# Gate and up of a SwiGLU by Strassen's seven products, their product through DRAM, on one Trainium2 core

## The chip, the cores and the metric

The kernel runs on one core of one Trainium2 chip. The metric is the device time of one execution in microseconds (us); less is better. Before the change the median of three runs is 2609.01 us (2608.06 to 2616.32). The core's engines are named as the profile names them: PE is TensorE's matmul, PEld its weight load, DVE is VectorE, ACT ScalarE, POOL GpSimd, and SP (SyncE) issues all the DMAs here.

## The reference

One layer of a block that mixes a state-space branch and a long convolution, then a feed-forward part; 512 tokens, width 2048, feed-forward width 5632, all in float32. The change is in the feed-forward part:

```python
def swiglu(h, wg, wu, wd):
    return (jax.nn.silu(h @ wg) * (h @ wu)) @ wd

        x = x + g1 * rmsnorm(y, norm_mix_post[layer])
        h = modulate(x, norm_ffn_pre[layer], sh2, sc2)
        x = x + g2 * rmsnorm(swiglu(h, w_gate[layer], w_up[layer], w_down[layer]), norm_ffn_post[layer])
```

## The kernel before, in words

Everything is kept transposed: features on the 128 partitions, the 512 tokens along the free dimension. A matrix product runs in three matmuls of type float32r: each operand is split into a high part and the rest, and `mm3` (L185) adds high x high, high x low and low x high into one PSUM bank of 512 columns (`acc`, four banks).

**Weights.** `wload` (L159) loads 128 x 1024 numbers (eight stationary blocks of 128 x 128) by a DMA on SP into `raw` (L156, three buffers), ACT casts them to `whi` (L164) and DVE subtracts to get `wlo` (L79); three buffers each, of 4096 bytes a partition, in the pool wp. `push` (L193) loads the weights of one step at once and runs the matmuls of the step two pushes earlier, so two steps of weights are ahead of PE. `gemm` (L212) pushes two such halves for a tile of 128 outputs and 2048 inputs. Between groups of four stationary blocks it calls `pump` (L136), which runs `pace` steps of generators in `fillers`: small work of DVE, ACT and POOL that is laid between the matmuls.

**Moving operands.** The pool big has 32 tiles of 512 columns (2048 bytes a partition), h0 to h15 and l0 to l15, used in turn for the inputs of all projections (hh, hl; mh, mlo) and then for the feed-forward input fx (`fh`, `fl`). By these sizes a moving operand and its weights begin at the same place of a 128-byte grid. `wload_big` (L168) puts weights that are used twice into tiles of big.

**The stretch around the change.** The output projection of the mixer ends in `y_second` (L1212), first for tokens 0 to 255, then for 256 to 511. After each half a filler `junction` (L1190) norms and adds (yT is then the stream x after the mixer, kept to the end of the kernel), norms again, and writes that half of fx (`modulated`, L302). Then come gate and up. `gate_up(i, c0, c1)` (L1248) makes tile i of 44: 96 matmuls for gate, 96 for up, silu on ACT, product on DVE, split into `ah` and `al` (six tiles of each, NA = 6, in the pool fa). The first six tiles run in two halves of 256 tokens, since the second half of fx comes later. After that chunks of four tiles (NCHUNK = 11) alternate with `down` (L1281): for each of eight q, two output tiles of 512 columns take the chunk's four inputs, and DVE adds each result into `y2a` (ACT copies the first). `ada(1)` between tiles runs one step of a matrix-vector product on DVE whose weights are loaded through `raw` as well. The last chunk runs in two halves of 256 tokens, with most of its weights kept by `wload_big`; `finish` (L1306) norms, adds yT and stores.

**Order.** The kernel is written in the Tile framework, which puts in the waits and plans the order of each engine's instructions and of SP's DMAs; an engine then takes its own in that order, and an instruction that waits holds up those behind it on its engine.

Of the kernel before, what the change touches and what calls it, by code (L numbers as in the profile page):

```python
# [23 lines left out]
EPS = 1e-6  # L24
NA = 6
LEAD = 2
NSQ = 0
# [37 lines left out]
def block_kernel(ctx: ExitStack, tc: tile.TileContext, I: dict, out: bass.AP, dbg=None, stop=None):  # L65
# [32 lines left out]

    rsm.tile([128, 16], F32, name="pad1")
    uniq = [0]  # L100
# [24 lines left out]

    hh = [big.tile([128, 512], F32R, tag=f"h{k}", name=f"hh{k}") for k in range(KT)]
    hl = [big.tile([128, 512], F32R, tag=f"l{k}", name=f"hl{k}") for k in range(KT)]
    hx = [(hh[k], hl[k]) for k in range(KT)]
# [39 lines left out]
    def wload_big(ap, q):  # L168

        raw = wraw(ap)  # L170
        parts = []
        for i in range(2):
            o = i * 512
            hi = big.tile([128, 512], F32R, tag=f"h{q * 2 + i}", name=nm("bhi"))
            lo = big.tile([128, 512], F32R, tag=f"l{q * 2 + i}", name=nm("blo"))
# [882 lines left out]
    flush(I["w_out"][n, 0] for n in range(2))  # L1058
    mh = [big.tile([128, 512], F32R, tag=f"h{k}", name=f"mh{k}") for k in range(KT)]
    mlo = [big.tile([128, 512], F32R, tag=f"l{k}", name=f"ml{k}") for k in range(KT)]  # L1060
    for j in range(8):
# [108 lines left out]

    fa_cm = pool("fa")
    fa = fa_cm.__enter__()
    jn_cm = pool("jn", side="right")
    jn = jn_cm.__enter__()
    posc = fa.tile([128, 512], F32, tag="ah", bufs=NA, name="posc")
    pos = pos_load(jn, posc.rearrange("p (k c) -> p k c", k=8))
    xr = [jn.tile([128, 512], F32, name=f"xr{k}") for k in range(KT)]
# [12 lines left out]
    def junction(h, prs):  # L1190
# [3 lines left out]
        for k in range(KT):  # L1194
            stt(yT[k][:, sl], yT[k][:, sl], gp[:, k : k + 1], rx[:, sl], MUL, MUL)
            tt(nc.vector if k % 2 else nc.gpsimd, yT[k][:, sl], yT[k][:, sl], xr[k][:, sl], ADD)
            pr2.add(yT[k][:, sl])
            yield
        yield
        yield from rstd_steps(pr2, D, 2, rx[:, sl])  # L1200
        for k in range(KT):
            if h == 0:
                fx[k] = (big.tile([128, 512], F32R, tag=f"h{k}", name=f"fh{k}"),
                         big.tile([128, 512], F32R, tag=f"l{k}", name=f"fl{k}"))
            modulated(fx[k][0][:, sl], fx[k][1][:, sl], yT[k][:, sl], a2[:, k : k + 1], mod[:, 5, k : k + 1], rx[:, sl], 256)
            yield
# [38 lines left out]

    acts = {}

    def gate_up(i, c0, c1):  # L1248
# [3 lines left out]
        def up_done(pu):  # L1252
            if i not in acts:
                h = fa.tile([128, 512], F32R, tag="ah", bufs=NA, name=nm("ah"))
                l = fa.tile([128, 512], F32R, tag="al", bufs=NA, name=nm("al"))
                acts[i] = (h, l)
# [15 lines left out]
    jn_cm.__exit__(None, None, None)  # L1272
    ff_cm = pool("ff")
    ff = ff_cm.__enter__()
    y2a = ff.tile([128, 16, 512], F32, name="y2a")
    y2 = [y2a[:, n, :] for n in range(16)]
    pace[0] = 1
    for i in range(NA):
        gate_up(i, 256, 512)

    def down(c, q, c0, c1, done, w=None):  # L1281
        def run(wt):
            for s in range(2):
                n = q * 2 + s
                p = acc()[:, : c1 - c0]
                for k in range(4):
                    ah, al = acts[c * 4 + k]
                    mm3(p, *wt[s * 4 + k], ah[:, c0:c1], al[:, c0:c1], k == 0, k == 3)
                if c == 0:
                    nc.scalar.copy(out=y2[n][:, c0:c1], in_=p)  # L1290
                else:
                    tt(nc.vector, y2[n][:, c0:c1], y2[n][:, c0:c1], p, ADD)
                done(n)
# [3 lines left out]

    for c in range(NCHUNK):
        for i in range(max(c * 4 + NA - 4, NA), min(c * 4 + NA, 44)):
            gate_up(i, 0, 512)  # L1300
        for q in range(8 if c < NCHUNK - 1 else 0):
            down(c, q, 0, 512, lambda n: None)
    ada(1000)
    tt(nc.vector, gp, mod[:, 7, :], vec[:, V_FPOST : V_FPOST + 16], MUL)

    def finish(h, prs):  # L1306
        sl = slice(h * 256, h * 256 + 256)
        yield from rstd_steps(prs, D, 2, rx[:, sl])
        for n in range(0, 16, FG):
            y = y2a[:, n : n + FG, sl]  # L1310
            tt(nc.vector, y, y, rx[:, sl].unsqueeze(1).broadcast_to([128, FG, 256]), MUL)
            tt(nc.gpsimd if n // FG % FP in FQ else nc.vector, y, y, yTa[:, n : n + FG, sl], ADD)
            nc.sync.dma_start(out[n : n + FG, :, sl].rearrange("n p t -> p n t"), y)
# [22 lines left out]
    drain()  # L1336
    ff_cm.__exit__(None, None, None)
    fa_cm.__exit__(None, None, None)
    yt_cm.__exit__(None, None, None)

# [116 lines left out]
```

## Time and profile before

| what | value |
|---|---|
| median of three runs | 2609.01 us |
| profiled execution, its own time | 2608.6 us |
| its span, first to last instruction | 2606.8 us |
| mean granted clock of PE | 0.981 |
| PE busy | 2512.0 us (96%) |
| PEld busy | 2054.6 us (79%) |
| DVE busy | 1471.9 us (56%) |
| ACT busy | 759.4 us (29%) |
| POOL busy | 456.2 us (18%) |
| DMA | 388.52 MB, mean 149 GB/s |

Busy time is how long an engine had an instruction in it; matmuls overlap, so a row's mean of one matmul is longer than the distance between two starts. The chain of waits goes back from the last instruction to what released each step. [...]

### The profile page before, as it was taken

The numbers are of one execution on the slowest core, as the hardware profiler recorded it, in microseconds if no ns is written. First come the engines' busy times: TensorE is split into PE (matmuls) and PEld (weight loads), VectorE is DVE, ScalarE is ACT, GpSimd is POOL, SyncE is SP. The second block draws the span as 40 slices with busy tenths as digits, with TensorE's granted clock in tenths as the row PEclk, the third lists the DMA queues.
The fourth block names the chain that finished last, engine by engine and source line by source line (L and its number), as shares of the span: only waits on it lengthen the run. The fifth ranks groups of instructions, "written<-read, shape, count | busy, mean of one in ns | idle before, by whom it ended". The sixth has DMA issues, their size and how long they took to land.

```text
span 2606.8 us, 30938 instructions
## 1 busy us (share of the span) xinstructions
PE 2512.0 (96%) x12196; PEld 2054.6 (79%) x12196; DVE 1471.9 (56%) x1889; ACT 759.4 (29%) x1062; POOL 456.2 (18%) x421
## 2 busy tenths in 40 slices
PE   8999989899999999999999999999999999999997
PEld 3467779577767789999988888888888888888886
DVE  7986746888878767696334343434343333333335
ACT  3143325222123323455322222222222222222224
POOL 1130010665523245740000000000000000000005
PEclk9999999899999999999999999999999999999998
DMA  8867744444356666345433333333333333333332
GB/s 290 315 225 236 235 156 161 143 149 162 113 197 215 249 222 220 105 146 184 148 113 112 108 113 113 113 113 113 113 113 105 97 97 98 97 97 97 97 106 73
DMA packets 129354, 388.52 MB, mean 149 GB/s; under 512 B 13775, under 2 KB 34703, under 8 KB 127672
## 3 DMA queue, kind: packets, MB, share of 16 engines
q1 hardware_dynamic: 129208, 386.54, 45.3%
q8 instruction: 96, 1.57, 0.3%
q14 instruction: 50, 0.41, 0.0%
HBM read 367.09 MB, written 19.40 MB: 148 GB/s over the span
## 4 chain that ended last, share of the span: by engine, by line
PE 55%; DVE 2%; POOL 0%; issue 0%; ACT 0%; POOLq 0%; ACTq 0%; DVEq 0%
PE acc L82 55%; DVE y2a L79 1%; DVE yTa L76 0%; POOL gs L79 0%; PE aux L236 0%; PE aux L82 0%; DVE wlo L79 0%; DVE yTa L79 0%; ACT sq L73 0%; ACT whi L164 0%; POOLq L1452 0%; POOL r L79 0%; ACT dg L73 0%; POOL yTa L79 0%; ACT rx L279 0%
## 5 line engine op out<-in xcount | busy, mean ns | idle before, releaser
L164 ACT CAST whi<-raw 128x1024 fp32r<-128x1024 f32 (+1 forms) x436 | 453.2, 1040 | 1410.5 <-PE acc L82 1156.5
L79 DVE TENSOR_TENSOR wlo<-raw,whi 128x1024 fp32r<-128x1024 f32 x420 | 533.2, 1269 | 540.3 <-ACT whi L164 536.2
L82 PE MATMUL acc<-fh,wlo 128*128 128x512 f32 (+1 forms) x1600 | 583.2, 365 | 4.1 <-DVE wlo L79 4.1
L82 PE MATMUL acc<-fh,whi 128*128 128x512 f32 (+1 forms) x1600 | 583.6, 365 | 0.1
L82 PE MATMUL acc<-fl,whi 128*128 128x512 f32 (+1 forms) x1600 | 583.1, 365 | 0.0
L82 PEld LDWEIGHTS acc<-fh,wlo 128*128 128x128 f32 x1600 | 303.3, 190 | 51.9 <-DVE wlo L79 4.7
L82 PEld LDWEIGHTS acc<-fh,whi 128*128 128x128 f32 x1600 | 303.3, 190 | 47.9 <-ACT fh L73 0.3
L82 PEld LDWEIGHTS acc<-fl,whi 128*128 128x128 f32 x1600 | 303.3, 190 | 47.6 <-DVE fl L76 0.2
L79 POOL TENSOR_TENSOR gs<-gs,sq 128x256 f32<-128x256 f32 x91 | 86.7, 956 | 1432.1 <-ACT sq L73 1430.1
L82 PE MATMUL acc<-hh,whi 128*128 128x512 f32 x688 | 283.9, 415 | 4.3 <-ACT hh L73 4.1
L82 PE MATMUL acc<-hl,whi 128*128 128x512 f32 x688 | 276.9, 402 | 2.8 <-DVE hl L76 2.8
L82 PE MATMUL acc<-hh,wlo 128*128 128x512 f32 x688 | 274.9, 400 | 0.0
L76 DVE SCALAR_TENSOR_TENSOR ada<-raw,cc,ada 128x512 f32<-128x512 f32 x240 | 199.1, 830 | 114.4 <-DMA raw<-in_ada 111.1
L82 PE MATMUL acc<-ah,whi 128*128 128x512 f32 (+1 forms) x688 | 262.7, 382 | 0.0
L82 PE MATMUL acc<-ah,wlo 128*128 128x512 f32 (+1 forms) x688 | 262.5, 382 | 0.0
L82 PE MATMUL acc<-al,whi 128*128 128x512 f32 (+1 forms) x688 | 262.4, 382 | 0.0
L79 DVE TENSOR_TENSOR y2a<-y2a,acc 128x512 f32<-128x512 f32 (+1 forms) x176 | 112.1, 638 | 199.6 <-PE acc L82 199.4
L82 PEld LDWEIGHTS acc<-hh,whi 128*128 128x128 f32 x688 | 133.1, 194 | 40.1 <-ACT hh L73 6.0
L82 PEld LDWEIGHTS acc<-hh,wlo 128*128 128x128 f32 x688 | 133.0, 193 | 33.9 <-issue 4.5
L82 PEld LDWEIGHTS acc<-hl,whi 128*128 128x128 f32 x688 | 133.1, 193 | 33.8 <-DVE hl L76 3.8
L82 PEld LDWEIGHTS acc<-ah,whi 128*128 128x128 f32 x688 | 129.3, 188 | 25.2
L82 PEld LDWEIGHTS acc<-al,whi 128*128 128x128 f32 x688 | 129.3, 188 | 25.0
(297 smaller groups left out, 3084.1 us busy)
## 6 DMA issues: line engine op xcount, KB each, us to landing
raw<-in_ada SPq DMA_DIRECT2D x128, 512.0 KB, 3.8
raw<-in_w_gate SPq DMA_DIRECT2D x100, 512.0 KB, 3.5
raw<-in_w_up SPq DMA_DIRECT2D x100, 512.0 KB, 3.5
raw<-in_w_down SPq DMA_DIRECT2D x88, 512.0 KB, 3.5
ada<-in_ada SPq DMA_DIRECT2D x64, 512.0 KB, 5.0
raw<-in_w_hy SPq DMA_DIRECT2D x44, 512.0 KB, 3.8
raw<-in_w_out SPq DMA_DIRECT2D x41, 512.0 KB, 4.4
raw<-in_w_xbc SPq DMA_DIRECT2D x38, 512.0 KB, 3.3
```

The source lines that it names most:

```text
L76: nc.vector.scalar_tensor_tensor(out=o, in0=a, scalar=s, in1=b, op0=op0, op1=op1)
L79: e.tensor_tensor(out=o, in0=a, in1=b, op=op)
L82: nc.tensor.matmul(o, lhsT, rhs, start=start, stop=stop)
L164: nc.scalar.copy(out=hi[:, :n], in_=raw[:, :n])
```

## The change

**Gate and up by pairs of tiles.** The first six tiles stay as they are. The other 38 are taken in 19 pairs, gate and up each: a block of 256 outputs (two tiles) x 2048 inputs (two halves) times 2048 inputs x 512 tokens (two halves) is a 2 x 2 by 2 x 2 product of blocks. `quad` makes it in seven block products of 128 x 1024 by 1024 x 256, in the form with few additions, and not in eight. Four sums of the moving blocks are made once (`sums_of_x`, a filler beside the second halves of the first six tiles; split into th and tl), four sums of the weights for each block on DVE before the cast. The seven results lie in four PSUM banks; `early` and `end` combine them into R on DVE and ACT, then silu, then the product with gate.

**The product goes through DRAM.** It is stored to `hd` (also that of the first six tiles) and loaded again by `act_load` for down, two tiles a DMA, then split. yT is stored to `x1d` in the junction, its space is given to the sums and weights, and `finish` loads it again through three tiles.

**Down in three chunks.** Chunks 0 to 4 and 5 to 9 each are summed in PSUM over 20 inputs; chunk 10 runs as before. ada steps run in the first of these.

**Operands 64 bytes apart.** The tiles of big are 576 columns wide and used from column 16, fx from column 0; wp begins with a pad of 64 bytes; pads in rsm and fd follow. So fx, th and tl begin 64 bytes off their weights on the 128-byte grid, the other operands of big do not.

```diff
-    rsm.tile([128, 16], F32, name="pad1")
+    rsm.tile([128, 64], F32, name="pad1")
+    wp.tile([128, 16], F32, name="pad2")
...
+    def block(tag, name, o=16):
+        return big.tile([128, 576], F32R, tag=tag, name=name)[:, o : o + 512]
...
+            nc.sync.dma_start(x1d[k][:, sl], yT[k][:, sl])
             yield
...
-                fx[k] = (big.tile([128, 512], F32R, tag=f"h{k}", name=f"fh{k}"),
-                         big.tile([128, 512], F32R, tag=f"l{k}", name=f"fl{k}"))
+                fx[k] = (block(f"h{k}", f"fh{k}", 0), block(f"l{k}", f"fl{k}", 0))
...
-            split(acts[i][0][:, c0:c1], acts[i][1][:, c0:c1], sg[:, :n])
-            if n == 512:
-                ada(1)
+            nc.sync.dma_start(hd[i][:, c0:c1], sg[:, :n])
...
+    def sums_of_x():
+        for k in range(8):
+            xb = gu.tile([128, 4, 256], F32, tag="ra", bufs=4, name=nm("xb"))
+            tb = gu.tile([128, 4, 256], F32, tag="ra", bufs=4, name=nm("tb"))
+            for i, q in enumerate((k, k + 8)):
+                tt(nc.vector, xb[:, 2 * i : 2 * i + 2, :].rearrange("p a b -> p (a b)"),
+                   fx[q][0].bitcast(F32), fx[q][1].bitcast(F32), ADD)
+            yield
+            tt(nc.vector, tb[:, 0:4:2, :], xb[:, 1:4:2, :], xb[:, 0:2, :], SUB)
+            tt(nc.vector, tb[:, 1, :], xb[:, 3, :], tb[:, 0, :], SUB)
+            tt(nc.vector, tb[:, 3, :], tb[:, 1, :], xb[:, 2, :], SUB)
+            yield
+            th = gu.tile([128, 4, 256], F32R, tag=f"th{k}", name=f"th{k}")
+            tl = gu.tile([128, 4, 256], F32R, tag=f"tl{k}", name=f"tl{k}")
+            split(th, tl, tb)
+            tx.append((th, tl))
+            yield
...
+    def feed(raw, body):
+        hi = wp.tile([128, 1024], F32R, tag="whi", bufs=3, name=nm("whi"))
+        lo = wp.tile([128, 1024], F32R, tag="wlo", bufs=3, name=nm("wlo"))
+        nc.scalar.copy(out=hi, in_=raw)
+        if pend:
+            pend.pop()()
+        pend.append(lambda: tt(nc.vector, lo, raw, hi.bitcast(F32), SUB))
+        for op in late:
+            op()
+        late.clear()
+        ahead.append(([(hi[:, c : c + 128], lo[:, c : c + 128]) for c in range(0, 1024, 128)], body))
+        if len(ahead) > 2:
+            w, fn = ahead.pop(0)
+            fn(w)
...
+        def early():
+            p12, p75, p6 = ps[0], ps[2], ps[4]
+            nc.scalar.copy(out=R[:, 0, :], in_=p12[:, 0:256])
+            tt(nc.vector, R[:, 0, :], p6[:, 0:256], R[:, 0, :], SUB)
+            tt(nc.vector, R[:, 2, :], R[:, 0, :], p75[:, 0:256], SUB)
+            tt(nc.vector, R[:, 1:4:2, :], R[:, 0:4:2, :], p75[:, 256:512].unsqueeze(1).broadcast_to([128, 2, 256]), ADD)
+            nc.scalar.copy(out=R[:, 0, :], in_=p12[:, 0:256])
+            tt(nc.vector, R[:, 0, :], R[:, 0, :], p12[:, 256:512], ADD)
+
+        def end():
+            tt(nc.vector, R[:, 1:3, :], R[:, 1:3, :], ps[5].rearrange("p (a b) -> p a b", a=2), SUB)
...
+                tt(nc.vector, R[:, 0, :], R[:, 0, :], g[:, 0, :], MUL)
+                stt(R[:, 1, :], R[:, 1, :], -1.0, g[:, 1, :], MUL, MUL)
+                tt(nc.vector, R[:, 2:4, :], R[:, 2:4, :], g[:, 2:4, :], MUL)
+                nc.sync.dma_start(hd[m1 : m1 + 2].rearrange("m p t -> p m t"), R.rearrange("p (m a) b -> p m (a b)", m=2))
...
+        feed(r11, body(0))
+        feed(r12, body(1))
+        tt(nc.vector, r11, r11, r21, ADD)
+        feed(r11, body(2))
+        tt(nc.vector, r21, r21, r22, ADD)
+        feed(r21, body(3))
...
+        tt(nc.vector, r11, r11, r22, ADD)
+        feed(r11, body(4))
...
+        feed(r22, body(5))
+        tt(nc.vector, r11, r11, r12, ADD)
+        feed(r11, body(6))
...
+    def act_load(i):
+        raw = fd.tile([128, 2, 512], F32, tag="st", bufs=3, name=nm("st"))
+        nc.sync.dma_start(raw, hd[i : i + 2].rearrange("m p t -> p m t"))
+        for b in range(2):
...
+            split(h, l, raw[:, b, :])
+            acts[i + b] = (h, l)
...
+    for g, (ca, cb) in enumerate(((0, 5), (5, 10))):
...
+                if g == 0:
+                    ada(1)
+                down_piece(c, q, ps, c == ca, c == cb - 1, done)
...
+        x1 = [y2p.tile([128, FG, 256], F32, tag="x1", bufs=3, name=nm("x1"))]
+        nc.sync.dma_start(x1[0], x1d[0:FG, :, sl].rearrange("n p t -> p n t"))
```

`body(i)` runs the 24 matmuls of product i, each of 256 columns; each `feed` is one cast, one subtraction and the matmuls of the product two feeds earlier.

## Rows read from the trace of the kernel before

**Rows 1.** The page: busy time by engine, and the granted clock in 40 slices.
```profile
PE 2512.0 (96%) x12196; PEld 2054.6 (79%) x12196; DVE 1471.9 (56%) x1889; ACT 759.4 (29%) x1062; POOL 456.2 (18%) x421
...
PEclk9999999899999999999999999999999999999998
```

**Rows 2.** The chain that ended last: start us, us, what.
```profile
1168.70 298.10 PE acc L82 x1716
...
1467.58 261.29 PE acc L82 x1152
...
1991.73 567.37 PE acc L82 x2592
...
2591.54 9.92 DVE y2a L79 x11
```

**Rows 3.** Busy time of each engine by stretch, granted clock, DMA share, GB/s.
```profile
core 0: us, PE busy (x) PEld busy (x) DVE busy (x) ACT busy (x) POOL busy (x), PEclk, DMA share, GB/s
0.00:40.00 40.00, 33.58 (x64) 9.60 (x64) 25.76 (x44) 19.44 (x35) 4.74 (x9) 1.00 0.84 309
...
1151.00:1159.00 8.00, 4.44 (x32) 4.00 (x32) 8.00 (x10) 3.71 (x7) 7.20 (x8) 0.98 0.21 68
1159.00:1163.00 4.00, 4.00 (x24) 4.00 (x24) 3.62 (x6) 2.33 (x6) 1.42 (x2) 0.62 0.49 135
...
1190.00:1270.00 80.00, 80.00 (x669) 80.00 (x668) 42.15 (x50) 34.95 (x46) 0.00 (x0) 1.00 0.58 183
1270.00:2535.00 1265.00, 1265.00 (x5597) 1048.14 (x5597) 462.86 (x501) 292.31 (x326) 0.00 (x0) 1.00 0.34 106
```

**Rows 4.** Timeline of PE, matmuls of 256 columns: start us, us, what.
```profile
1119.62 0.28 PE L82 MATMUL acc<-fh,whi 128*128 128x256 f32 x1
...
1120.94 0.28 PE L82 MATMUL acc<-fh,wlo 128*128 128x256 f32 x1
```

**Rows 5.** Groups by line and shape, 1300 to 2535: count, busy us, mean ns.
```profile
L82 PE MATMUL acc<-fh,whi 128*128 128x512 f32 x1215 | 473.0, 389 | 0.0
...
L79 DVE TENSOR_TENSOR wlo<-raw,whi 128x1024 fp32r<-128x1024 f32 x227 | 278.0, 1225 | 397.1 <-ACT whi L164 397.1
L164 ACT CAST whi<-raw 128x1024 fp32r<-128x1024 f32 x226 | 238.3, 1054 | 948.3 <-PE acc L82 866.1 <-issue 82.1
...
L79 DVE TENSOR_TENSOR y2a<-y2a,acc 128x512 f32<-128x512 f32 x144 | 99.1, 688 | 185.8 <-PE acc L82 185.5
...
L79 DVE TENSOR_TENSOR al<-sg,ah 128x512 fp32r<-128x512 f32 x37 | 25.3, 685 | 0.0
L181 ACT CAST ah<-sg 128x512 fp32r<-128x512 f32 x37 | 22.8, 617 | 0.0
```

**Rows 6.** Timeline of PE, a pair of tiles of another part.
```profile
535.24 0.40 PE L82 MATMUL acc<-hh,wlo 128*128 128x512 f32 x1
535.48 0.39 PE L82 MATMUL aux<-arh,mr 128*128 128x512 f32 x1
...
536.17 0.40 PE L82 MATMUL aux<-arl,mr 128*128 128x512 f32 x1
```

**Rows 7.** Groups by line and shape, 1165 to 1270: steps of 256 columns.
```profile
L79 DVE TENSOR_TENSOR sg<-sg,acc 128x256 f32<-128x256 f32 x9 | 3.8, 421 | 5.5 <-PE acc L82 5.5
...
L73 ACT ACTIVATE sg<-acc 128x256 f32<-128x256 f32 x9 | 3.4, 377 | 0.9 <-DVE fl L76 0.9
```

**Rows 8.** DMA issues of the whole run: count, KB each, us to landing.
```profile
raw<-in_w_gate SPq DMA_DIRECT2D x100, 512.0 KB, 3.5
...
out_dram<-y2a SPq DMA_DIRECT2D x16, 256.0 KB, 2.2
...
ut<-udr SPq DMA_DIRECT2D x8, 256.0 KB, 2.7
```

**Rows 9.** DMA issues from 1300 to 2535.
```profile
raw<-in_ada SPq DMA_DIRECT2D x21, 512.0 KB, 3.5
```

**Rows 10.** Timeline of DVE in the junction: start us, us, what.
```profile
1172.71 0.88 DVE L76 SCALAR_TENSOR_TENSOR fl<-mt,mod,fh 128x256 fp32r<-128x256 f32 x2
1173.50 0.88 DVE L76 SCALAR_TENSOR_TENSOR mt<-yTa,a,rx 128x256 f32<-128x256 f32 x2
...
1176.22 0.48 DVE L76 SCALAR_TENSOR_TENSOR mt<-yTa,a,rx 128x256 f32<-128x256 f32 x1
```

**Rows 11.** Timeline of SP's queue, a store and the load behind it.
```profile
386.37 0.33 SPq L535 DMA_DIRECT2D udr<-hv  x1
387.50 0.33 SPq L156 DMA_DIRECT2D raw<-in_w_xbc  x1
```

**Rows 12.** Waits of SP's queue: total us, times, longest us.
```profile
SPq L535 <- DVE hv L79: 13.0, 7, 7.0
```

More of the change, by code (lines that the diff above doesn't have):

```diff
@@ L124, in block_kernel @@
     act(cc, cc, AF.Silu)
-    hh = [big.tile([128, 512], F32R, tag=f"h{k}", name=f"hh{k}") for k in range(KT)]
-    hl = [big.tile([128, 512], F32R, tag=f"l{k}", name=f"hl{k}") for k in range(KT)]
+    def block(tag, name, o=16):
+        return big.tile([128, 576], F32R, tag=tag, name=name)[:, o : o + 512]
+    hh = [block(f"h{k}", f"hh{k}") for k in range(KT)]
+    hl = [block(f"l{k}", f"hl{k}") for k in range(KT)]
     hx = [(hh[k], hl[k]) for k in range(KT)]
@@ L173, in wload_big @@
             o = i * 512
-            hi = big.tile([128, 512], F32R, tag=f"h{q * 2 + i}", name=nm("bhi"))
-            lo = big.tile([128, 512], F32R, tag=f"l{q * 2 + i}", name=nm("blo"))
+            hi = block(f"h{q * 2 + i}", nm("bhi"))
+            lo = block(f"l{q * 2 + i}", nm("blo"))
             split(hi, lo, raw[:, o : o + 512])
@@ L1058, in block_kernel @@
     flush(I["w_out"][n, 0] for n in range(2))
-    mh = [big.tile([128, 512], F32R, tag=f"h{k}", name=f"mh{k}") for k in range(KT)]
-    mlo = [big.tile([128, 512], F32R, tag=f"l{k}", name=f"ml{k}") for k in range(KT)]
+    mh = [block(f"h{k}", f"mh{k}") for k in range(KT)]
+    mlo = [block(f"l{k}", f"ml{k}") for k in range(KT)]
     for j in range(8):
@@ L1272, in block_kernel @@
     jn_cm.__exit__(None, None, None)
[L1273 to L1276, printed above, removed]
+    yt_cm.__exit__(None, None, None)
+    gu_cm = pool("gu")
+    gu = gu_cm.__enter__()
+    tx = []
+    def sums_of_x():
[15 more added lines that the diff above has]
+            yield
+    fillers.append(sums_of_x())
     pace[0] = 1
@@ new lines, in block_kernel @@
+    todo = [list(q) for q in quads()]
+    todo[0] += [qload("ra", I[todo[0][1]][2 * todo[0][0], i]) for i in range(2)]
+    for n, q in enumerate(todo):
+        quad(*q, todo[n + 1] if n + 1 < len(todo) else None)
+    while pend:
+        pend.pop()()
+    first = [wload(I["w_down"][0, 0])]
+    for op in late:
+        op()
+    late.clear()
+    w, fn = ahead.pop(0)
+    fn(w)
+    first.append(wload(I["w_down"][1, 0]))
+    for op in late:
+        op()
+    late.clear()
+    w, fn = ahead.pop(0)
@@ new lines, in down_piece, with run, early_loads @@
+    def down_piece(c, q, ps, first, last, done):
+        def run(wt):
+            for s in range(2):
+                if first:
+                    ps.append(acc())
+                for k in range(4):
+                    ah, al = acts[c * 4 + k]
+                    mm3(ps[s], *wt[s * 4 + k], ah, al, first and k == 0, last and k == 3)
+                if last:
+                    done(q * 2 + s, ps[s])
+            pump()
+        push(I["w_down"][c, q], run)
+    def early_loads(i0, i1):
+        for i in range(i0, i1, 2):
+            act_load(i)
+            yield
@@ new lines, in block_kernel, with done @@
+    for g, (ca, cb) in enumerate(((0, 5), (5, 10))):
+        def done(n, p, g=g):
+            if g == 0:
+                nc.scalar.copy(out=y2[n], in_=p)
+            else:
+                tt(nc.vector, y2[n], y2[n], p, ADD)
+        for q in range(8):
+            ps = []
+            if g == 0 and q == 6:
+                fillers.append(early_loads(20, 26))
+            if g == 1 and q == 6:
+                fillers.append(early_loads(40, 44))
+            for c in range(ca, cb):
+                if q == 0:
+                    for i in range(c * 4, c * 4 + 4, 2):
+                        if i not in acts:
+                            act_load(i)
+                if g == 0:
+                    ada(1)
+                down_piece(c, q, ps, c == ca, c == cb - 1, done)
@@ L1281, in down @@
+    drain([I["w_down"][NCHUNK - 1, 0], I["w_down"][NCHUNK - 1, 1]])
+    ada(1000)
+    tt(nc.vector, gp, mod[:, 7, :], vec[:, V_FPOST : V_FPOST + 16], MUL)
     def down(c, q, c0, c1, done, w=None):
```

111 lines of the change are left out of this document (87 added, 24 removed).

## The prediction

> **What bounds the kernel now.** I read the page first: TensorE (PE) is busy 96% of the span, the other engines far less, and the granted clock is 0.8 or more in every slice [rows 1]. A busy PE need not be a fast one, so next I read the chain of waits: from 1168.70 to 2559.09 it is PE alone, and 1152 matmuls take 261.29 us there, 226.8 ns each [rows 2]. [...] So in gate, up and down the number of matmuls times their spacing is the time, and DVE and ACT have room. The profiled execution took 2608.6 us; the median of the runs is 2609.01, so I take the sum against 2608.6. A measurement of this kernel can tell about 0.3% (7.8 us) from no change.
>
> **Spacing.** With 256 columns starts are 120.0 ns apart (1119.62 to 1120.94 is 11 steps) [rows 4]. Both sizes together: 226.8 - 120.0 = 106.8 ns for 256 columns, so each matmul pays 13.2 ns that do not grow with its columns. Halving the columns pays this twice. That is the first thing the change gives away.
>
> **Gate and up, the main term.** Before, 38 tiles (6 to 43) run in one sweep: 38 x 2 matrices x 16 x 3 = 3648 matmuls of 512 columns (the view counts 1215 of each of the three kinds) [rows 5], 3648 x 226.8 = 827.4 us. After, 19 pairs x 2 x 7 products x 8 x 3 = 6384 matmuls of 256 columns. Seven of eight would give 12.5%; at 120.0 ns it is 766.1 us, 61.3 us or 7.4% less.
>
> **Operands 64 bytes apart.** By the code's sizes (tiles of 2048 bytes in big, 4096 in wp) moving operand and weights now begin on the same place of a 128-byte grid; afterwards fx, th and tl (and ch and cl of the context, too few to count) stand 64 bytes off whi and wlo; the others do not. No row shows such a pair, so I bound the spacing s. Below: the 13.2 ns vanish, 106.8. Above: matmuls of another pair of tiles of the same form (arh, arl on mr) start 232.5 ns apart (535.24 to 536.17, four steps) [rows 6], 5.7 more than the rest, so 126. Those rows show that the 13.2 is not fixed, and 120 lies between the ends. I take 117, since the nearest row is 120 and the room below it is twice that above. Then 6384 x 117 = 746.9, a gain of 80.5 us; the ends give 145.6 and 23.0. The first six tiles (1152 matmuls of 256 columns, before and after) add 1152 x 3 ns = 3.5 us (ends +15.2 and -6.9).
>
> [...]
>
> **What hides the new DVE work.** A block of seven products takes PE 7 x 24 x 120 = 20.2 us. Its DVE work: seven wlo and four weight sums at 1.225 us [rows 5] make 13.5; three combining steps of 256 columns at 0.42 [rows 7] and two of 512 at 0.69 [rows 5] make 2.6; the products of silu(gate) and up, in every second block, 0.42 + 0.42 + 0.69, on average 0.8. Sum 16.9 of 20.2 us (19.7 at s = 117), so throughput holds. The tight place is the wait for product 5 of a block: the combining starts when it ends, and weights three ahead are needed when the two products already loaded are through, 5.8 us later. Cast 1.05 [rows 5], an ACT copy 0.38, three DVE steps 0.42 + 0.42 + 0.69 [rows 5, 7], copy 0.38, step 0.42, wlo 1.22: 5.0 us. Cost 0 with 0.8 to spare; were it gone, 38 blocks wait. The store of each pair's product waits on SP for DVE; behind it stand two loads for the next block, needed a block (20 us) later: 0. The splits of the product (ACT 0.617, DVE 0.685 a tile [rows 5]) only move, from gate and up to down.
>
> **Sums of x.** 24 filler steps run under the second halves of the six tiles. DVE for each of eight k: two of 512 at 0.69, one more of 512, two of 256, a split of 1.22: 4.1, together 33 us. PE needs 576 x 120 = 69 us there; DVE was busy 42 of 80 [rows 3], of which six splits al (0.42) go. 42 - 3 + 33 = 72 against 69: full. The steps come in the first half (four to a matrix tile), so PE waits about 5 us (0 to 12).
>
> **The turn to down.** All of the product comes back from DRAM: 44 tiles of 256 KB, two to a load. The first blocks h0 to h7 come free after product 1 of the last block, some 17 us early, the staging tiles once the last weight sums are split, so a load (3.5 us for 512 KB [rows 8]), a cast 0.61 and a split 0.69 [rows 5] lie mostly beside the last products. If the first load has to stand behind the last store of the product it is 2.2 (a 256 KB store [rows 8]) + 3.5 + 1.3 + the end of the block 2.2 = 9 us, and PE's clock falls in such a gap: after a stretch of 4.4 busy us in 8 it was 0.62 [rows 3]. I take 5 (0 to 16). Then the first q: five pieces of 5.44 us want 5 MB of product, 2.5 MB of weights, and 2.5 MB of ada weights (21 such loads are left [rows 9]): 10 MB in 27 us is 370 GB/s; the best stretch moved 309 [rows 3]. 10 / 0.309 = 32 us, of which some is loaded early: 4 us (0 to 10). The second group has no ada: 276 GB/s, 0.
>
> **Down in three chunks**: as many matmuls of 512 columns as before. 144 or more DVE additions go (0.688 each [rows 5]); PE had no gap beside them [rows 3], so 0. **x1 through DRAM**: 32 stores on SP's queue in the junction. What orders a queue is not the code's order alone: the code says mt, fl for each k, DVE ran them fl, fl, mt, mt [rows 10]. So I expect no store to stand ahead of a weight load that could go; 1 us for SP's issues (0.33 each [rows 11], beside PE). **Finish**: the last 9.92 us [rows 2] are eight steps of 1.24; three x1 tiles give a load 3.7 us against the 2.7 of a 256 KB load [rows 8]. I take 2 for both halves (0 to 6).
>
> **Sum**: -80.5 - 3.5 + 5 + 5 + 4 + 1 + 2 = -67; 2608.6 - 67 = **2542 us**.
>
> **Rivals.**
> (a) The whole 13.2 ns goes in gate and up. For: the surplus is equal at 256 and 512 columns, so it belongs to the change of weights, where two reads can meet; against: no row of such a pair. At 106.8: -145.6 - 15.2 + 17, and with blocks of 17.9 us DVE (16.9) is nearly full and the 5.0 us chain meets a lead of 5.1, so +10: 2475. [...]
> (b) The 5.0 us chain outlasts its lead: semaphores between these eight steps, or DVE taking them in another order. For: 0.8 us of room; against: the order on DVE is planned [rows 10], so a wlo may be put ahead. One us a block is 38 us; at s = 120 that is -61.3 + 17 + 38, **2602**: no change.
> (c) Slower: SP's queue goes by code order in the junction, and each weight load stands behind the x1 stores before it. For: SP waited up to 7.0 us for the tile of a store [rows 12], and this stretch already starves PE (4.44 of 8 us) [rows 3]; against: the planned order above. Price: 1.8 steps to a load, each stt 0.48 [rows 10] and add 0.42 [rows 7], then load 3.5, cast 1.05, wlo 1.22: 7.4 us where PE has work for 2.9, so 4.5; 14 loads (9 in the second half, 5 in the first, where seven tiles keep their weights) are 63 us, and the 12 stores of the first tiles' product hold a load 1.2 each (0.38 + 0.42 + 0.33 + 3.5 + 1.05 + 1.22 = 6.9 against two loads of work, 5.8): together 77, 2619 with the forecast's gain. It decides from 15 held loads.
> The distance doing nothing (s = 120) is 2608.6 - 61.3 + 17 = 2564, inside the forecast's case.
>
> **Numbers.** Forecast 0.49 (2520 to 2575), (a) 0.24, (b) 0.13, (c) 0.14. (b) falls half in the band of no change; of (c) a fifth. Faster 0.49 + 0.24 + 0.06 = 0.79, same 0.10, slower 0.11. The range reaches (a) and (b): 2474 to 2604, leaving out most of (c).
>
> **What would show it.** In the profile after: 6384 matmuls from fx, th, tl with starts near 117 ns and no idle time of PE before them (waits on wlo there mean (b)); a gap of about 5 us before the first matmul of down; the DMA rate of the first q near 300 GB/s; PE's gap in the junction as before (raw loads a few us apart; more is (c)). The forecast is wrong if spacing leaves 110 to 124, or the turns cost over 30 us.

## The result, and the profile of the changed kernel

The changed kernel took **2536.0 us** (median of 4 runs, 2534.33 to 2562.26) against 2612.21 us for the kernel before beside it: a ratio of **0.9727**, 95% interval 0.967 to 0.9784. Forecast were 2542 us, with a range of 2474 to 2604. The total is close, in part by luck: in most executions the block products gained 24 us more than forecast, and the smaller terms together cost some 17 us more. The experiments below are mostly about those two errors.

One thing has to be known before any profile of this kernel is read. Its executions fall into two groups: of the ten timed here (four, and six of a repeat below), seven took 2525.5 to 2536.6 us, with a median of 2534.3, and three 2562.3 to 2565.3. The profiled execution is of the upper group: 2562.26 us, span 2560.4.

The page of the changed kernel: busy time by engine and granted clock (PEclk, the share of full speed that the profile gives for PE) [rows 1].

```profile
PE 2436.5 (95%) x14932; PEld 2118.2 (83%) x14932; DVE 1802.5 (70%) x2278; ACT 914.5 (36%) x1273; POOL 458.5 (18%) x421
...
PEclk9999999999899999999999999999999899999998
```

DVE went from 56% to 70%, PE holds 95%, and the clock has a dip that it had not before, in slice 32 of 40: that is the turn to down. Next the busy time by stretch [rows 3]: the junction, the sums of x, the block products, the turn's gap, and the first 48 matmuls of down.

```profile
core 0: us, PE busy (x) PEld busy (x) DVE busy (x) ACT busy (x) POOL busy (x), PEclk, DMA share, GB/s
1129.00:1177.00 48.00, 40.57 (x309) 39.03 (x310) 38.36 (x55) 23.31 (x44) 24.33 (x23) 0.93 0.58 183
1228.00:1240.00 12.00, 10.19 (x84) 9.67 (x82) 12.00 (x18) 7.03 (x9) 0.00 (x0) 1.00 0.40 134
1280.00:2029.00 749.00, 749.00 (x6362) 749.00 (x6361) 602.21 (x659) 324.01 (x397) 0.00 (x0) 1.00 0.35 118
2029.00:2044.50 15.50, 3.04 (x27) 2.84 (x26) 10.10 (x17) 3.15 (x5) 0.00 (x0) 0.70 0.82 267
2044.50:2057.80 13.30, 13.30 (x51) 10.55 (x51) 9.91 (x15) 7.11 (x12) 0.00 (x0) 0.84 0.92 330
```

The block products run without a gap: 6362 matmuls in 749.00 us, 117.7 ns each, and DVE has 147 us to spare. Before, the same work took 827.4 us. Then PE stands still for 12.5 of the 15.5 us, the clock falls (0.70 in that stretch, 0.84 in the next), and 48 matmuls that take 10.9 us at the spacing of before (48 x 226.8 ns) take 13.3. The list of PE's waits from 1280 to 2060 has that one entry and no other:

```profile
PE acc L83 <- ACT ah L187: 12.5, 1, 12.5
```

What SP's queue did meanwhile (timeline of SP, start, us, what):

```profile
2023.03 6.49 SPq L162 DMA_DIRECT2D raw<-in_ada  x3
2031.47 0.33 SPq L162 DMA_DIRECT2D raw<-in_w_down  x1
2034.34 0.38 SPq L1392 DMA_DIRECT2D hd<-R  x1
2035.00 0.33 SPq L162 DMA_DIRECT2D raw<-in_ada  x1
2038.64 0.33 SPq L162 DMA_DIRECT2D raw<-in_w_down  x1
2039.06 1.41 SPq L1451 DMA_DIRECT2D st<-hd  x3
```

The last matmul of gate and up starts at 2031.8. The first load of the product (`st<-hd`) goes out 4.7 us after the last store of the product (`hd<-R`), behind an ada load and a second weight load, and down begins at 2044.5. That last store's row among the DMA issues from 2029 to 2060, and the chain that ended last, from the cast of the first weights of down to its first matmuls:

```profile
hd<-R SPq DMA_DIRECT2D x1, 512.0 KB, 3.7
```

```profile
2036.31 1.05 ACT whi L170
2037.38 1.24 DVE wlo L80
2039.06 4.33 DMA st<-hd
2044.50 13.32 PE acc L83 x48
```

So the last store had landed at 2038.0, and the second weight load went out at 2038.64, when `wlo` of the first was done; the loads of the product stood behind it. The end of the run, from the same chain [rows 2]:

```profile
2541.43 3.57 DVE y2a L80 x4
2545.47 4.14 DMA x<-x1d
2550.44 1.27 POOL y2a L80
2552.16 3.63 DMA x<-x1d
2555.92 1.29 POOLq L1671
```

Before, the last eleven steps on DVE followed one another; now two loads of x1 stand between the steps. And the DMA issues [rows 8]:

```profile
st<-hd SPq DMA_DIRECT2D x22, 512.0 KB, 5.8
...
x<-x1d SPq DMA_DIRECT2D x16, 256.0 KB, 3.6
out_dram<-y2a SPq DMA_DIRECT2D x16, 256.0 KB, 2.6
```

### The profile page after: what moved, and what is told of

It reads as the page before. It is cut to its first block, busy times and chain, and to the rows that moved or that the text cites. A ratio compares the mean times of both kernels' runs of the same rounds, so it can differ in the third digit from the quotient of the medians.

```text
span 2560.4 us, 37510 instructions
## 1 busy us (share of the span) xinstructions
PE 2436.5 (95%) x14932; PEld 2118.2 (83%) x14932; DVE 1802.5 (70%) x2278; ACT 914.5 (36%) x1273; POOL 458.5 (18%) x421
## 4 chain that ended last, share of the span: by engine, by line
PE 51%; DVE 2%; issue 1%; POOL 1%; DMA 1%; ACT 1%; POOLq 0%; SPq 0%; ACTq 0%; DVEq 0%
PE acc L83 22%; PE acc L1361 10%; PE acc L1360 10%; PE acc L1362 10%; POOL gs L80 1%; DVE wlo L80 1%; DMA x<-x1d 0%; DVE y2a L80 0%; ACT whi L170 0%; POOL y2a L80 0%; PE aux L83 0%; DMA raw<-in_w_down 0%; POOL yTa L80 0%; DMA st<-hd 0%; POOL r L80 0%
## 5 line engine op out<-in xcount | busy, mean ns | idle before, releaser
L80 DVE TENSOR_TENSOR wlo<-rq,whi 128x1024 fp32r<-128x1024 f32 x266 | 323.8, 1223 | 122.7 <-ACT whi L1321 117.9
L1321 ACT CAST whi<-rq 128x1024 fp32r<-128x1024 f32 x266 | 279.0, 1049 | 358.8 <-PE acc L1361 318.6
L1360 PE MATMUL acc<-th,whi 128*128 128x256 f32 x1216 | 341.7, 281 | 0.0
L1361 PE MATMUL acc<-tl,whi 128*128 128x256 f32 x1216 | 341.7, 281 | 0.0
L1362 PE MATMUL acc<-th,wlo 128*128 128x256 f32 x1216 | 341.7, 281 | 0.0
L83 PE MATMUL acc<-ah,whi 128*128 128x512 f32 (+1 forms) x688 | 264.0, 384 | 12.5 <-ACT ah L187 12.5
L1360 PE MATMUL acc<-fh,whi 128*128 128x256 f32 x912 | 256.3, 281 | 0.0
L1361 PE MATMUL acc<-fl,whi 128*128 128x256 f32 x912 | 256.3, 281 | 0.0
L1362 PE MATMUL acc<-fh,wlo 128*128 128x256 f32 x912 | 256.3, 281 | 0.0
L1360 PEld LDWEIGHTS acc<-th,whi 128*128 128x128 f32 x1216 | 233.5, 192 | 0.0
L1361 PEld LDWEIGHTS acc<-tl,whi 128*128 128x128 f32 x1216 | 228.2, 188 | 0.0
```

Of the source, the lines that this page charges most:

```text
L80: e.tensor_tensor(out=o, in0=a, in1=b, op=op)
L83: nc.tensor.matmul(o, lhsT, rhs, start=start, stop=stop)
L1321: nc.scalar.copy(out=hi, in_=raw)
L1360: nc.tensor.matmul(p, wh, xh, start=k == 0, stop=False, skip_group_check=True)
L1361: nc.tensor.matmul(p, wh, xl, start=False, stop=False, skip_group_check=True)
L1362: nc.tensor.matmul(p, wl, xh, start=False, stop=k == 7, skip_group_check=True)
```

## The experiments

My theory after this profile: the distance of 64 bytes is worth what the spacing shows, the rest of the 26 us between executions lies in one stage, and the turn and the finish are matters of order and memory, not of bandwidth. Rivals stand in each expectation. All times are medians unless a range is given; the kernel before took 2610.8 to 2613.8 us beside them.

### The same kernel again

No edit.

> The changed kernel, unaltered, for a profile of a typical execution: the profiled execution shown with the change took 2562.26 us, 26 us over the median of 2536.0. If those 26 us belong to the turn to down or to the last stage, this profile shows those gaps shorter than 12.7 us and 75.6 us. If they are spread (every stage longer by about 1%), the stages are in proportion and the granted clock is higher than 0.977 on average. I expect 2536 us, the gate and up stretch at 117.5 ns a matmul again, and the turn's gap unchanged at 10 to 13 us.

Measured: 2534.11 us (2525.54 to 2565.26, 6 runs); the profiled one 2562.39. Turn and last stage are as in the first profile (gap 12.4 us), so they do not hold the 26 us. Two kernels that differ from this one only behind the block products (below) were profiled in the lower group, and there the difference is plain. The windows of the repeat, a piece of the second halves of the six tiles and then three pieces of the block products:

```profile
1180.00:1220.00 40.00, 40.00 (x355) 40.00 (x354) 38.93 (x63) 25.49 (x37) 0.00 (x0) 1.00 0.59 194
1300.00:1500.00 200.00, 200.00 (x1700) 200.00 (x1699) 161.86 (x179) 87.26 (x108) 0.00 (x0) 1.00 0.37 119
1500.00:1750.00 250.00, 250.00 (x2125) 250.00 (x2124) 200.05 (x218) 108.28 (x134) 0.00 (x0) 1.00 0.37 121
1750.00:2000.00 250.00, 250.00 (x2125) 250.00 (x2125) 203.17 (x225) 108.20 (x133) 0.00 (x0) 1.00 0.37 120
```

The same windows of turn_both, profiled at 2524.68 us:

```profile
1180.00:1220.00 40.00, 40.00 (x342) 40.00 (x341) 37.90 (x63) 24.21 (x34) 0.00 (x0) 1.00 0.57 186
1300.00:1500.00 200.00, 200.00 (x1767) 200.00 (x1766) 166.16 (x181) 89.85 (x110) 0.00 (x0) 1.00 0.38 125
1500.00:1750.00 250.00, 250.00 (x2208) 250.00 (x2208) 209.74 (x233) 111.85 (x136) 0.00 (x0) 1.00 0.38 126
1750.00:2000.00 250.00, 250.00 (x2209) 250.00 (x2208) 210.84 (x233) 115.14 (x144) 0.00 (x0) 1.00 0.37 122
```

250 / 2125 = 117.6 ns in the one, 250 / 2208 = 113.2 ns in the other, at the same clock of 1.00, without a wait in either, and unchanged from the first window of the block products to the last. (A window also counts the two or three matmuls that reach over its ends; from start to start the trace has 117.8 and 113.3.) The difference, 6384 x 4.4 = 28 us, is the distance between the two groups. The expectation had neither of its two guesses right: the 26 us are all in one stage, and it is the one that I had taken for settled. The first window adds that the level does not belong to the execution: the repeat has 40 / 355 = 112.7 ns there (113.3 from start to start) and 117.6 later, turn_both 117.0 (117.8) and then 113.2. Between the two windows the stream of matmuls is broken: PE waits for `wlo` twice in the repeat (3.1 us together) and once in turn_both (2.1 us), and around these waits some starts are 0.2 to 0.35 us apart.

### The distance between operands: 0, 32 and 96 bytes

```diff
-fx[k] = (block(f"h{k}", f"fh{k}", 0), block(f"l{k}", f"fl{k}", 0))
+fx[k] = (block(f"h{k}", f"fh{k}", o), block(f"l{k}", f"fl{k}", o))
 gu = gu_cm.__enter__()
+gu.tile([128, o], F32, name="padg")
```

with o = 16 (0 bytes from the weights), 24 (32 bytes) and 8 (96 bytes).

> The moving operands of gate and up (fh, fl, th, tl) are put on the same place of the 128-byte grid as the weights, as all pairs were in the kernel before; nothing else changes. If the distance makes the spacing (117.4 ns at 64 bytes against 120.0 at 0), 6384 + 1152 matmuls of 256 columns pay 2.6 ns more each: +19 us, 2555 us, and the stretch of block products 766 us instead of 749. If the distance does nothing and the 117.4 ns has another cause (the way the block products are written), the time stays 2536 and the stretch 749.

> The moving operands of gate and up stand 32 bytes behind the weights' place on the 128-byte grid (64 in the changed kernel). Shown so far: at 0 the block products start 120.0 ns apart in every profile; at 64 they start 113.3 ns apart in some executions and 117.5 in others, the same from first to last of a stretch of 730 us, which makes the 26 us between executions of one kernel. If what matters is only that the distance is not 0, 32 gives the same two levels, 113.3 and 117.5: 2525 to 2536, now and then 2562. If the two reads meet in slots of the grid, 32 is another case: before, tiles 32 apart took 5.7 ns more than the rest at 512 columns, so about 126 ns, +50 to +80 us, 2590 to 2610.

> The same with 96 bytes (32 ahead of the next place). If the two reads meet in slots, 96 behaves as 32 does, only mirrored, and both runs show one and the same spacing, between 117.5 and 126 ns. If only zero is special, it shows 113.3 and 117.5 again. A level of its own below 113.3, with one value in all executions, would make it the better distance.

Measured: 2578.53 us at 0 (2571.81 to 2584.28, 5 runs; ratio 0.9877, 0.9858 to 0.9896), 2556.49 at 32 (2552.69 to 2561.76, 5 runs), 2566.71 at 96 (2562.13 to 2572.11, 4 runs). None of the three has two groups. One window of the block products each, first apart0, then d32, then d96:

```profile
1500.00:1750.00 250.00, 250.00 (x2085) 250.00 (x2085) 199.53 (x218) 106.84 (x134) 0.00 (x0) 1.00 0.35 114
```

```profile
1500.00:1750.00 250.00, 250.00 (x2145) 250.00 (x2144) 203.56 (x226) 108.48 (x132) 0.00 (x0) 1.00 0.37 121
```

```profile
1500.00:1750.00 250.00, 250.00 (x2115) 250.00 (x2114) 199.23 (x218) 107.39 (x131) 0.00 (x0) 1.00 0.38 123
```

119.9, 116.6 and 118.2 ns. So the distance is the cause of the shorter spacing: with nothing moved but the tiles' place, 0 bytes gives back the 120.0 of the kernel before [rows 4]. Neither operand's own place does it: by the addresses of the built kernels fx begins at byte 0 of the 128-byte grid both before (weights at 0) and in the change (weights at 64), and apart0 has both at 64. The distance is worth 6.7 ns a matmul at the lower level (6384 x 6.7 = 43 us; 2578.5 - 2534.3 = 44) and 2.3 at the upper. My expectation of 2555 for apart0 was low because I had priced it from the one upper profile. For 32 and 96 both ends were wrong: they are neither as good as 64 nor the 126 that I had scaled from [rows 6]. That row was no case of 32 bytes: by the built kernel's addresses arh, arl and mr all begin at byte 96 of the grid, 0 apart, and over the whole trace the steps from arh to arl take 229.6 ns on average, not 232.5. In both new runs single steps spread, over 112 to 121 ns at 32 bytes and 115 to 124 at 96, and their mean holds still.

### The same distance for all large matmuls

The tiles hh, hl, mh, mlo and the activations of down also begin at the place 0 (`block(..., 0)`, no `pad3`), 64 bytes off the weights.

> All large matmuls get the 64 bytes, not those of gate and up alone: the moving operands of the first stages, of the output projection and of down. Theory: the surplus goes with the weights that are read beside a moving operand, so it falls at 512 columns by as much as at 256: 226.8 to between 224.3 and 220.1 ns. With 1920 such matmuls in the two groups of down and some 1800 of the first stages, and some 1300 of 256 columns in the output projection and the last stage, that is 3720 x 2.5 to 6.7 = 9 to 25 us, and 1300 x 2.5 to 6.7 = 3 to 9 us: 2502 to 2524 against 2536. Rival: at 512 columns the surplus is another one (232.5 ns was measured there at 32 and 96 apart), and down stays at 226.8; the time falls by under 5 us.

Measured: 2551.36 us (6 runs: four at 2546.4 to 2551.9, two at 2574.1 and 2581.1): slower than the change in either group (2534.3, and 2562.3 to 2565.3), not faster. Down, 2200 to 2480, first in the repeat of the changed kernel (0 bytes there), then here (64 bytes):

```profile
2200.00:2480.00 280.00, 280.00 (x1237) 231.86 (x1236) 84.09 (x83) 67.52 (x76) 0.00 (x0) 1.00 0.33 109
```

```profile
2200.00:2480.00 280.00, 280.00 (x1202) 226.19 (x1201) 82.91 (x82) 65.90 (x74) 0.00 (x0) 1.00 0.32 105
```

226.4 and 232.9 ns: at 512 columns 64 bytes cost 6.5 ns where at 256 they save 2 to 7. Both my theory and its rival (226.8, unchanged) fall. The change was right to keep the distance from the matmuls of 512 columns. It could have gone further with those of 256: in this run's trace the unbroken steps of the output projection at 256 columns take 116.5 ns on average, where the changed kernel has 119.9.

### A level chosen at each gap?

```diff
+for _ in range({10: 8, 19: 10, 28: 12}.get(n, 0)):
+    nc.scalar.copy(out=q[2], in_=q[2])
 quad(*q, todo[n + 1] if n + 1 < len(todo) else None)
```

> Three times in the block products (before blocks 10, 19 and 28 of 38) the weights of the next product are copied onto themselves 8, 10 and 12 times by ScalarE before their cast, so that PE runs dry for some us and the stretch without a gap is cut into four. At 64 bytes apart a stretch so far ran at 113.3 or at 117.5 ns from its first to its last matmul, and executions differ by 26 to 28 us. Theory: the level is chosen anew whenever PE starts after a gap and then stays; then the four parts of one execution are not all of one level, and the times of several executions lie at steps of about 7 us (6384 x 4.2 ns / 4) between the two ends. Rival: the level belongs to the execution (all four parts alike, and the times fall into two groups 26 us apart again), or it drifts with time and not with gaps. The gaps themselves add about 1, 3 and 5 us and some clock.

Measured: 2548.6 us; three runs at 2530 to 2537 and three at 2561 to 2563. The edit made no gap: PE is busy 700 of the 700 us from 1300 to 2000, so all 30 copies (31.4 us of ACT) found room. The run therefore does not test the question, and shows only that two groups remain when no gap is made. That the level can change where the stream is broken rests on the two executions above. It fits the other profiles: in the ten at 64 bytes the steps of the block products average 113.3 ns (turn_both, finish8, best1, best3) or 117.8 (the other six), nothing between, and none changes within the block products. What picks the level was not found.

### The combining chain of a block

Three more copies ahead of the first step of `early` (R block 0 from the same PSUM columns).

> Three more copies on ScalarE (0.38 us each) stand at the head of each block's combining chain, 38 times, so the chain from the end of product 5 to the split of the next weights is 1.1 us longer. The prediction gave that chain 5.0 us against a lead of 5.8 at 120 ns, and 1 us a block as the price of each us over. Theory by that count: at 113.3 ns the lead is 5.4 us, the chain 6.1, PE waits 0.7 us in each of 38 blocks: +27 us. Rival: DVE does the split of the weights ahead of the chain's steps, since its order is not the code's, so PE does not wait at all and the time is the same within 3 us.

Measured: 2547.98 us (2534.39 to 2563.67, 6 runs), in two groups again: 2534.4 to 2540.3 and 2555.7 to 2563.7. The profiled one took 2563.67 against 2562.39 for the repeat, and PE is busy 745.00 of the 745 us from 1285 to 2030. At this spacing, 117.8 ns, the rival holds; at 113.3, for which the theory was worked out, no profile was taken, and the three runs lie 0 to 6 us over the change's 2534.3 where the theory has 27. The groups of ACT say why:

```profile
L1321 ACT CAST whi<-rq 128x1024 fp32r<-128x1024 f32 x263 | 275.8, 1049 | 312.6 <-PE acc L1361 280.6 <-DVE R L80 32.0
```

Of the 312.6 us for which ACT idled before a cast, 280.6 went on PE giving back a weight tile and 32.0 on DVE's steps on R, which are the chain. So the preparation of the next weights mostly waits for a free tile and not for the chain, as my count of 5.0 us against 5.8 had it.

### The turn to down

First without the ada loads in the first q, and with the first four tiles of the product loaded in staging tiles of the weights:

```diff
+for i in (0, 2):
+    act_split(i, qload("raw", hd[i : i + 2].rearrange("m p t -> p m t")),
+              [(block(f"h{s}", nm("ah")), block(f"l{s}", nm("al"))) for s in (i, i + 1)])
 first = [wload(I["w_down"][0, 0])]
...
-if g == 0:
+if g == 0 and q > 0:
     ada(1)
```

> The turn to down: the first four tiles of the product are loaded into staging tiles of the weights and before the first two weight tiles of down, not after them and in memory of the stage before, and the ada loads leave out the first q. Theory: the 12.7 us gap is the order on SP's queue (ada, hd store, ada, weight, then the loads of the product), so the gap falls to under 4 us and the first 48 matmuls run at full clock (10.9 instead of 13.3 us): 10 to 13 us less, about 2524. Rival: the load must wait for the last store of the product anyway or DMA is the limit (330 GB/s in the first q); then the gap is only moved into the first q and the time falls by under 4 us.

Measured: 2527.73 us; by groups 2521.6 to 2530.8 and 2552 to 2561.6. The lower group's median, 2524.3, is 10 us under the change's 2534.3 (its runs 4 to 13). PE goes into down without a gap, starts 24 matmuls and then waits 5.2 us. In the first 100 us after the last block product PE started 417 matmuls, 385 in the repeat of the changed kernel (first row here: the repeat; second: turn_both; third: best3, below):

```profile
2032.20:2132.20 100.00, 87.63 (x385) 71.99 (x385) 62.12 (x84) 34.37 (x48) 0.00 (x0) 0.93 0.81 277
```

```profile
2001.30:2101.30 100.00, 94.81 (x417) 77.95 (x416) 57.11 (x76) 33.21 (x45) 0.00 (x0) 0.97 0.74 254
```

```profile
2005.40:2105.40 100.00, 95.38 (x415) 78.83 (x415) 58.05 (x76) 33.17 (x45) 0.73 (x1) 0.97 0.76 254
```

32 matmuls at 0.227 are 7.3 us, which is what the trace shows of the 10; the theory had 10 to 13, the rival under 4. But the gap did not fall under 4 us, and what was left of it is a wait of SP, in its queue's waits from 2000 to 2008:

```profile
SPq L1461 <- DMA hd<-R: 1.6, 1, 1.6
```

The first load of the product in a staging tile of down goes out at 2006.58, as the last store lands. Next the store of each pair's product went to POOL's queue (`nc.gpsimd.dma_start(hd[...], R...)`), together with the finish of the next section:

> The turn's two parts (first product tiles loaded in staging tiles of the weights, no ada loads in the first q), with the store of each pair's product issued by GpSimd instead of SP, and the earlier x1 loads of the last stage. With the first two alone the gap before down is 5.2 us instead of 12.5 and comes 24 matmuls later, when SP, which had to wait for the last store of the product (2003.49), issues the next loads of the product at 2006.58. Theory: with the store on another queue those loads go ahead of it and the gap falls to under 2 us; with the last stage at 72 us instead of 75.5, about 2522 where the spacing is 113.3 (2534 for the changed kernel there). Rival: the staging tiles lie where the weights' sums of the block products are, and are not free before the end in any case: the gap stays at 5 us, 2525.

Measured: **2521.86 us** (2519.3 to 2523.0, 4 runs), ratio 0.9654 (0.9639 to 0.967), all four in the lower group by their times; the change there took 2534.3, so the edits of the turn and of the finish together give 12 us. The gap stayed at 5.3 us, and SP, which no longer issues the store, still waits for it to land (2004 to 2012):

```profile
SPq L1461 <- DMA hd<-R: 2.7, 1, 2.7
```

So it is not the queue that holds the loads here. Last, R got a pool of its own, and the two edits of the junction came in:

```diff
+rp_cm = pool("rp", side="right")
+rp = rp_cm.__enter__()
...
-R = gu.tile([128, 4, 256], F32, tag="R", bufs=2, name=nm("R"))
+R = rp.tile([128, 4, 256], F32, tag="R", bufs=2, name=nm("R"))
```

> best1, with the result tiles R of the block products in memory of their own, so that the staging tiles of down no longer wait until the last store of the product has landed (with that store on GpSimd's queue the loads still went out 4.0 us after it, at 2010.64, and the gap stayed at 5.3 us). Also in it: the x1 stores of the junction on ScalarE's queue, and the sums of x at half the pace over all of the second halves. Theory: the staging tiles' memory is what the loads wait for; the gap before down falls from 5.3 us to under 2. The junction and sums give 2 to 6 us. Together 2513 to 2518 where the spacing is 113.3. Rival: the loads wait for the last matmuls that read the memory, or for DMA; the gap stays at 4 to 5 us.

Now the loads go out before the last block product starts its last matmul (2005.3), and the wait for `ah` is gone:

```profile
2002.93 1.60 SPq L1465 DMA_DIRECT2D st<-hd  x3
```

So it was the pool. The staging tiles of down do not lie where R lay: by the built kernels' addresses they take bytes 132160 to 144448 of a partition, in this run too, and R had 214016 to 222208. But they take memory of the pool gu, R was a tile of gu, and the loads waited until R's last store had landed; with R in another pool they do not. In these kernels the framework put in this wait by pool, not by address. The time is not gone, though; it turns up further on, as the only wait of PE from 1990 to 2160:

```profile
PE aux L83 <- DVE ada L77: 4.6, 1, 4.6
```

The third row above has 95.38 busy us of 100 where turn_both has 94.81, but 415 matmuls started where turn_both has 417: nothing is won. Product, weights and ada share the queue; the chain into this wait goes through a load of the product that took 7.22 us, and about 5 us of lateness moved from one consumer to the next. best3 took 2541.96 us (7 runs: two at 2516.4 and 2525.1, five at 2538.4 to 2544.7); the profiled one, 2525.1, has 113.3 ns. The five look like its upper group, where the change takes 2562 to 2565, but none of them was profiled. Whether it beats best1 in the lower one, two runs do not settle.

### The last stage

```diff
-x1 = [y2p.tile([128, FG, 256], F32, tag="x1", bufs=3, name=nm("x1"))]
-nc.sync.dma_start(x1[0], x1d[0:FG, :, sl].rearrange("n p t -> p n t"))
+x1 = x1s[h]
...
+if q == (4, 6)[h]:
+    x1_load(h)
```

`x1_load` loads a half's x1 in four pieces of 512 KB, three in the staging tiles of down.

> The last stage: x1 of each half is loaded as four loads of 512 KB before the half's sums of squares are complete (at q 4 and 6 of the last chunk), so no step of the finish waits for x1. Theory: the finish's tail is 20.2 us from the last product where it was 15.2 in the kernel before, because each step waits for an x1 load; it falls by 4 to 5 us, to about 2531. Rival: the tail is set by the stores of the output (2.6 us each) and by DVE and POOL in turn, and the time stays within 1 us.

Measured: 2530.07 us; by groups 2527.0 to 2530.5, 4 to 7 under the change's 2534.3, and 2558.9 and 2563.1, which can't be told from its 2562.3 to 2565.3. The end of its chain has no load of x1 in it any more:

```profile
2510.58 1.24 PE aux L83 x2
...
2513.46 2.43 DVE y2a L80 x3
...
2516.34 5.83 DVE y2a L80 x6
2522.28 1.60 POOLq L1682
```

From the last matmul of down that reads the activations to the end it is 21.0 us, with the change 26.1, before 20.7. The theory holds.

### The junction and the sums of x

```diff
-nc.sync.dma_start(x1d[k][:, sl], yT[k][:, sl])
+nc.scalar.dma_start(x1d[k][:, sl], yT[k][:, sl])
...
-pace[0] = 1
+pace[0] = 0.5
```

> The changed kernel with two edits up to the block products, each in a stretch of its own: the 32 x1 stores of the junction are issued by ScalarE instead of SP, and the sums of x run at half the pace. Theory: the stores stand among the weight loads on SP's queue, and that is why PE is busy 40.6 of the 48 us from 1129 to 1177 where it had shorter gaps before; off the queue, PE gains 2 to 4 us there, and the gap of 2.35 us at 1238 goes: 2530 to 2532 at the lower spacing. Rival: the gaps are those of DVE and ScalarE (normalising, modulating, splitting), the queue has nothing to do with them, and ScalarE's issues delay its casts: the first matmul of the block products comes at the same time or later, 2534 to 2538.

Measured: 2557.11 us (2525.18 to 2564.82, 6 runs), four runs in the upper group, which makes the median useless; the stretches tell more (columns as above):

```profile
1125.00:1280.00 155.00, 147.25 (x1219) 145.88 (x1219) 134.76 (x191) 82.00 (x117) 25.97 (x23) 0.98 0.61 198
1129.00:1177.00 48.00, 41.02 (x319) 39.74 (x317) 39.61 (x57) 24.64 (x45) 25.97 (x23) 0.93 0.58 184
1228.00:1240.00 12.00, 12.00 (x104) 12.00 (x103) 12.00 (x17) 6.24 (x7) 0.00 (x0) 1.00 0.57 194
```

The gap of the sums is gone (12.00 busy us instead of 10.19), as the theory said, and the six tiles, from their first matmul to the first of the block products, take 150.6 us instead of 154.5. In the junction PE starts 319 matmuls where three profiles with the stores on SP start 309, 311 and 309 (the change, the repeat, finish8), about 1 us; its 41.02 busy us lie among their 40.57, 38.74 and 42.26. Taking the stores off SP's queue did little there, as the rival had it.

## Why the prediction came out right, point by point

The sum had one large term and six small ones. In the larger group of executions the block products take 6384 x 113.2 = 722.7 us, a gain of 104.7 where I had 80.5. Everything else then costs 2534.3 - 2608.6 + 104.7 = 30 us, where I had 13.5 (-3.5 + 5 + 5 + 4 + 1 + 2). The two errors, -24 and +17, nearly cancel: that the total came within 6 us is luck, though each term that had ends lay within them. apart0 checks this without any doubt about levels: its block products gain 827.4 - 6384 x 119.9 = 62 us, its profiled time is 31.1 under that of before, so the rest costs 31 there too; for that very case I had written 2564, and it took 2578.5.

Where the rest went, by the profiles of before and of the change: the six tiles begin 5.9 us later; they take 154.5 us where they took 151.2 (3.3; forecast, with spacing, sums and stores, 2.5); the turn costs 12.5 and 2.4 us of clock; the last stage 4.5. That is 28.6 us, and nearly all that the two spans leave for it.

- **Spacing.** That halving the columns gives away part of the gain was right (119.9 at 0 bytes). "I take 117" failed as one number: at 64 bytes there are two levels, 113.2 and 117.6, and the nearest row could not show it. Both lie within my bounds of 106.8 and 126, but the bounds were poorly founded. "13.2 ns that do not grow" came out of two sizes and two unknowns, so it could not be tested; at 64 bytes the two sizes move in opposite directions (119.9 to 113.2 or 117.6 ns at 256 columns, 226.4 to 232.9 at 512). And the upper bound came from a pair that is 0 bytes apart (above).
- **The distance doing nothing** (s = 120, 2564 us) is not what the runs show: with nothing moved but the tiles' place, s is 119.9 at 0 bytes, 116.6 at 32, 118.2 at 96 and 113.2 or 117.6 at 64. Why is not shown.
- **DVE beside the block products.** Cost 0 was right; PE has no wait there in any profile. The tight place that I named for it was not tight at 117.8 ns (chain3).
- **Sums of x.** 5 forecast; one wait of 2.1 us ends at 1240.3, and half the pace removes it.
- **x1 stores and junction.** 1 forecast. The first matmul of the six tiles starts 5.9 us later than before [rows 4] (now 1125.5); of that, 2.6 is there at the start of the output projection already, a place where the profiles of these kernels lie anywhere from 877 to 888. From 1119 to 1180 PE's waits are 8.0 us where they were 4.7. The stores on SP are not the cause of it (7.7 in junct); what is stays open.
- **The turn.** This step failed most: 5 taken, 12.5 of gap plus 2.4 of lost clock measured. The case that I had worked out (the first load behind the last store, 9 us) was the one that happened. Two things held the load there: its place on SP's queue behind a weight load, which had the last word in the changed kernel by 1 us, and, once that was moved, the pool that it takes its memory from, which I had not seen. The last store took 3.7 us to land; my 2.2 was that of a store half as large. It all still lies within the 0 to 16 given.
- **The first q.** 4 forecast, 0 measured, and PE does not wait again before 2500. That the gap before it had let the loads run ahead is my reading, not shown. With the gap away a wait of 4.6 us appears in best3. It is not quite the one that I had forecast, since best3 asks for no ada in its first q.
- **Down in three chunks.** 0 forecast, and 0 as far as the windows show: 226.4 ns a matmul without a wait from 2200 to 2480, 226.8 before.
- **Finish.** 2 forecast, 4.5 measured (the last stage took 71.1 us, now 75.6), and shown to be the x1 loads (finish8). The eight steps that I divided 9.92 us into are eleven on DVE in that row [rows 2].
- **Rivals.** (a) would need 106.8; no window lies under 112.7. That its surplus belongs to the change of weights, and that two reads meet there, was my guess; no run shows either. (b) and (c) name real dependencies, but the chain costs nothing at 117.8 ns (chain3). For the stores' tiles SP waited 19.2 us between 1119 and 1180, and yet only one cast of ACT waited for a load there, 1.7 us; (c) needed 15.

## What to carry to other kernels

The spacing of matmuls is a quantity to be measured for each pair of widths and places: a distance that saves up to 6.7 ns at 256 columns costs 6.5 at 512. A product sent through DRAM was paid at the turn, with a gap of 12.5 us here: the first loads can stand behind other loads on their queue (about 1 us of it), and can wait until a pool whose memory they take has seen its last store land (a gap of 5.3 us in best1). Look for both, give the stored tile a pool of its own, and look where the lateness goes next. And where executions of one kernel fall into groups, compare stretches within a group, not medians.

## What the chip showed that was not expected

At 64 bytes and 256 columns PE runs at one of two spacings, 113.2 or 117.6 ns, each held for over 700 us without a gap; it makes 28 us between executions of one and the same program. Both occur within one execution, in stretches that breaks in the stream of matmuls divide. At 0, 32 and 96 bytes no second group was seen in 4 to 5 runs each. What decides between the two was not found; a kernel that could choose the lower one would save about 28 us in some of its executions.
